# One joint small piece of 1260 columns instead of two of 840, in an L2 pooling kernel

## The chip, the cores and the metric

The kernel runs on one core of a Trainium2 chip. The metric is the device time of one execution in microseconds, lower is better. Before the change it was 394.82 us (median of 3 runs, 394.81 to 395.2). In what follows DVE is the VectorE, ACT the ScalarE, SP the SyncE. A "DMA engine" is one of the core's sixteen; a "row" is one DMA packet, the contiguous bytes of one partition (52,736 B for a load of 13184 columns).

## The reference, cut to what matters

```
x: [32, 256, 4096] float32, p = 2, kernel_size = 4
out[b, c, i] = ( mean over j < 4 of |x[b, c, 4 i + j]| ** p ) ** (1 / p)      # [32, 256, 1024]
```

Because windows of four neighbours never cross a row, the kernel treats the input as one flat list: 262144 columns on each of 128 partitions. Each element is squared, four neighbours are added, and the root of a quarter of the sum is taken. That is 134.2 MB in and 33.6 MB out, and little arithmetic.

## The kernel before

Twenty large loads go through three input buffers in turn: 18 of 13184 columns, then 12764, then 10388. ACT squares a load in place, DVE sums fours into one of two output buffers, ACT takes the root, and the result is stored, two loads to a store. The last loads are cut into chunks so that the work behind the last byte is short.

```python
W, O_W = 13184, 6592
slots = [[(W, [W])]] * 17 + [[(W, [6592, 6592])]]
slots += [[(12764, [5372, 7392])], [(10388, [6172, 2808, 1408])]]   # the last load: three chunks
ODD, ODD2 = 840, 840                                                 # the small pieces
...
# First small piece: 30 partitions x 3584 columns, the first thing that is loaded.
t = o_tiles[1][0:Q, 0:odd]                                           # Q = 30
by_load.append(nc.sync.dma_start(out=t, in_=...))
nc.vector.tensor_tensor(out=t, in0=t, in1=t, op=mult)
nc.vector.tensor_reduce(out=o, in_=t by fours, op=add)
nc.scalar.activation(out=o, in_=o, func=Act.Sqrt, scale=1.0 / k)
stores["odd"] = nc.scalar.dma_start(out=..., in_=o)                  # on the ACT queue
...
load(0)                                                              # the first large load
# Second small piece: 60 partitions (30 to 89) x 1792 columns, behind the first large load.
t2 = o_tiles[1][30:90, 0:ODD2 * P // 60]
by_load.append(nc.sync.dma_start(out=t2, in_=...))
load(1); load(2)
...                                                                  # t2 squared and summed likewise
# behind the square of load 0:
nc.scalar.activation(out=o2, in_=o2, func=Act.Sqrt, scale=1.0 / k)
stores["odd2"] = nc.sync.dma_start(out=..., in_=o2[30:90, :])        # on the SP queue
```

The small pieces hold the columns that the large loads leave over. The first is also a start: it gives the DMA engines something short to move before the first large load.

## Time and profile before

| what | before |
|---|---|
| time, median | 394.82 us |
| profiled span | 392.4 us |
| DVE busy, ACT busy | 277.4 us, 275.2 us |
| DMA over the span | 428 GB/s |
| first square on ACT begins | 20.70 us |
| last store is issued | 384.68 us |

The prediction below shows the lines and reads them. From about 6 us to 389 us the sixteen DMA engines hardly rest (16 rows or more are in flight in 99.7% of that time).

### The profile page before, as it was taken

To read this page: it belongs to the slowest core of one execution; us is meant where nothing else is said; L and a number is where in the kernel's file an instruction comes from. 1 tells how busy PE (TensorE), PEld (TensorE's weight loads), DVE (VectorE), ACT (ScalarE), POOL (GpSimd) and SP (SyncE) were. 2 spreads that over 40 slices of the span, in tenths; PEclk is the share of its full clock that TensorE was granted. 3 is DMA by queue.
4 is the path that set the end of the run, shared out by engine and by line. 5 is a ranking of instruction groups with operands and counts; after the bars stand their busy time and mean duration, and the time that the engine had idled before them with its cause. 6 is when DMAs were issued, how large, how long until landed. Compare 5 with 4: busy or idle time off the path is not lost.

```text
span 392.4 us, 186 instructions
## 1 busy us (share of the span) xinstructions
DVE 277.4 (71%) x38; ACT 275.2 (70%) x39; POOL 0.2 (0%) x4
## 2 busy tenths in 40 slices
DVE  4247698976678567856795769467947690889991
ACT  1084959927991899189908990899099909996991
POOL 0000000000000000000000000000000000000000
DMA  8999999999999999999999999999999999999997
GB/s 313 430 480 430 430 436 435 430 390 470 430 430 395 465 430 427 425 438 430 430 430 430 430 435 427 454 446 422 430 465 430 401 433 473 424 416 421 420 434 336
DMA packets 4704, 167.77 MB, mean 428 GB/s; under 512 B 556, under 2 KB 616, under 8 KB 706
## 3 DMA queue, kind: packets, MB, share of 16 engines
q1 hardware_dynamic: 3651, 144.04, 85.2%
q10 hardware_dynamic: 1053, 23.73, 14.0%
HBM read 134.22 MB, written 33.55 MB: 428 GB/s over the span
## 4 chain that ended last, share of the span: by engine, by line
DMA 50%; DVE 24%; ACT 22%; another core or an unknown queue 1%; SPq 0%; issue 0%
DMA xt<-in_x_dram 50%; ACT xt L185 21%; DVE ot L114 18%; DVE xt L125 3%; DVE xt L182 1%; ACT xt L105 1%; DVE xt L127 1%; DVE ot L127 0%; SPq L135 0%; SPq L154 0%; SPq L83 0%
## 5 line engine op out<-in xcount | busy, mean ns | idle before, releaser
L185 ACT ACTIVATE xt<-xt 128x13184 f32<-128x13184 f32 (+5 forms) x23 | 217.1, 9443 | 96.8 <-DMA xt<-in_x_dram 96.8
L114 DVE TENSOR_REDUCE ot<-xt 128x3296 f32<-128x13184 f32 x15 | 208.3, 13886 | 75.6 <-ACT xt L185 75.6
L105 ACT ACTIVATE ot<-ot 128x6592 f32<-128x6592 f32 x9 | 51.1, 5680 | 0.0
L125 DVE TENSOR_TENSOR xt<-xt 128x6592 f32<-128x6592 f32 (+6 forms) x9 | 34.1, 3786 | 16.2 <-ACT xt L185 16.0
L127 DVE TENSOR_TENSOR ot<-xt 128x3296 f32<-128x3296 f32 (+1 forms) x4 | 10.9, 2733 | 0.1
L158 DVE TENSOR_TENSOR ot<-ot 90x1792 f32<-90x1792 f32 x1 | 2.0, 2022 | 9.6 <-DMA ot<-in_x_dram 9.6
L142 ACT ACTIVATE ot<-ot 30x896 f32<-30x896 f32 x1 | 0.9, 948 | 10.7 <-DVE ot L138 10.7
L136 DVE TENSOR_TENSOR ot<-ot 30x3584 f32<-30x3584 f32 x1 | 3.9, 3878 | 4.9 <-DMA ot<-in_x_dram 4.9
L127 DVE TENSOR_TENSOR xt<-xt 128x1343 f32<-128x1343 f32 (+4 forms) x5 | 6.8, 1365 | 0.2
L105 ACT ACTIVATE xt<-xt 128x3191 f32<-128x3191 f32 (+3 forms) x4 | 5.6, 1406 | 1.2 <-DVE xt L127 1.2
L182 DVE TENSOR_TENSOR xt<-xt 128x5372 f32<-128x5372 f32 x1 | 5.7, 5748 | 0.0
L138 DVE TENSOR_REDUCE ot<-ot 30x896 f32<-30x3584 f32 x1 | 3.9, 3874 | 0.0
L159 DVE TENSOR_REDUCE ot<-ot 90x448 f32<-90x1792 f32 x1 | 2.0, 2016 | 0.0
L142 ACT ACT_TABLE_LOAD x1 | 1.3, 1283 | 0.7 <-PEq L226 0.7
L190 ACT ACTIVATE ot<-ot 90x448 f32<-90x448 f32 x1 | 0.6, 560 | 0.0
L226 POOL MEMSET const-bfloat16-1.0<- 128x1 bf16 x1 | 0.1, 102 | 0.0
L226 POOL MEMSET const-uint8-127<- 128x1 uint8 x1 | 0.1, 102 | 0.0
L226 POOL MEMSET const-float32-0.0<- 128x1 f32 x1 | 0.1, 99 | 0.2 <-issue 0.2
L226 POOL MEMSET const-float32-1.0<- 128x1 f32 x1 | 0.1, 99 | 0.0
## 6 DMA issues: line engine op xcount, KB each, us to landing
xt<-in_x_dram SPq DMA_DIRECT2D x18, 6592.0 KB, 31.3
out_dram<-ot ACTq DMA_DIRECT2D x7, 3296.0 KB, 27.2
out_dram<-ot SPq DMA_DIRECT2D x2, 3296.0 KB, 23.1
xt<-in_x_dram SPq DMA_DIRECT2D x1, 6382.0 KB, 32.0
xt<-in_x_dram SPq DMA_DIRECT2D x1, 5194.0 KB, 22.9
out_dram<-xt SPq DMA_DIRECT2D x1, 1595.5 KB, 10.8
out_dram<-xt SPq DMA_DIRECT2D x1, 1298.5 KB, 6.8
ot<-in_x_dram SPq DMA_DIRECT2D x2, 420.0 KB, 12.3
```

Of the source, the lines that this page charges most:

```text
L105: r = nc.scalar.activation(out=o, in_=o, func=Act.Sqrt, scale=1.0 / k)
L114: r = nc.vector.tensor_reduce(out=o, in_=v.rearrange("p (n j) -> p n j", j=k), axis=mybir.AxisListType.X, op=add,)
L125: r = nc.vector.tensor_tensor(out=h, in0=q[:, :, 0:2], in1=q[:, :, 2:4], op=add)
L127: r = nc.vector.tensor_tensor(out=o, in0=h[:, :, 0], in1=h[:, :, 1], op=add)
L136: nc.vector.tensor_tensor(out=t, in0=t, in1=t, op=mybir.AluOpType.mult)
L138: nc.vector.tensor_reduce(out=o, in_=t.rearrange("p (n j) -> p n j", j=k), axis=mybir.AxisListType.X, op=mybir.AluOpType.add,)
L142: nc.scalar.activation(out=o, in_=o, func=Act.Sqrt, scale=1.0 / k)
L158: nc.vector.tensor_tensor(out=t2, in0=t2, in1=t2, op=mybir.AluOpType.mult)
L159: r = nc.vector.tensor_reduce(out=o2, in_=t2.rearrange("p (n j) -> p n j", j=k), axis=mybir.AxisListType.X, op=mybir.AluOpType.add,)
L182: r = nc.vector.tensor_tensor(out=v, in0=v, in1=v, op=mybir.AluOpType.mult)
L185: r = nc.scalar.activation(out=v, in_=v, func=Act.Square)
L190: nc.scalar.activation(out=o2, in_=o2, func=Act.Sqrt, scale=1.0 / k)
```

## The change

The intent: use a shorter and better placed start. The two small pieces (840 + 840 columns) become one piece of 1260 columns, 90 rows of 7,168 B, whose first 30 rows are loaded ahead of the first large load and whose other 60 rows behind it. The piece is squared, summed, rooted and stored once. The 420 columns that are left go into the last large load, whose first chunk grows from 6172 to 6592 columns. The piece lies on partitions 2 to 91, so that its 60 rows begin at partition 32 (step 2 of the prediction has what the author estimated to gain by that). The instructions on it start at partition 0, so partitions 0 and 1 are cleared first by a memset.

```diff
-    slots += [[(12764, [5372, 7392])], [(10388, [6172, 2808, 1408])]]
-    ODD, ODD2 = 840, 840
+    slots += [[(12764, [5372, 7392])], [(10808, [6592, 2808, 1408])]]
+    ODD = 1260
...
-    (first piece: load, multiply, reduce, root, store on the ACT queue)
+    LOW, Q, FIRST = 2, 90, 30
+    odd = ODD * P // Q
+    t = o_tiles[1][:, 0:odd]
+    nc.vector.memset(t[0:LOW, :], 0.0)
+    by_load.append(nc.sync.dma_start(out=t[LOW:LOW + FIRST, :], in_=src[0:FIRST, :]))
...
         if ahead == 1:
-            t2 = o_tiles[1][30:90, 0:ODD2 * P // 60]
-            by_load.append(nc.sync.dma_start(out=t2, in_=...))
+            by_load.append(nc.sync.dma_start(out=t[LOW + FIRST:LOW + Q, :], in_=src[FIRST:Q, :]))
...
-    (second piece: multiply and reduce on partitions 0 to 89)
+    (the joint piece: multiply and reduce on partitions 0 to 91)
...
             if i == 0:
-                nc.scalar.activation(out=o2, in_=o2, func=Act.Sqrt, scale=1.0 / k)
-                stores["odd2"] = nc.sync.dma_start(out=..., in_=o2[30:90, :])
+                nc.scalar.activation(out=o_odd, in_=o_odd, func=Act.Sqrt, scale=1.0 / k)
+                stores["odd"] = nc.sync.dma_start(out=dst, in_=o_odd[LOW:LOW + Q, :])
```

More of the change, by code (lines that the diff above doesn't have):

```diff
@@ L55 @@
     n = len(loads)
-    assert sum(w for _, _, w, _ in loads) + ODD + ODD2 == total
+    assert sum(w for _, _, w, _ in loads) + ODD == total
     firsts = [sum(groups[:g]) for g in range(len(groups))]
@@ L129, in total_sum @@
         sums.append(r)
-    Q = 30
+    LOW, Q, FIRST = 2, 90, 30
     odd = ODD * P // Q
-    t = o_tiles[1][0:Q, 0:odd]
-    by_load.append(nc.sync.dma_start(out=t, in_=xf[(total - ODD) * P:total * P].rearrange("(p w) -> p w", p=Q)))
-    nc.vector.tensor_tensor(out=t, in0=t, in1=t, op=mybir.AluOpType.mult)
-    o = o_tiles[1][0:Q, odd:odd + odd // k]
-    nc.vector.tensor_reduce(
-        out=o, in_=t.rearrange("p (n j) -> p n j", j=k),
-        axis=mybir.AxisListType.X, op=mybir.AluOpType.add,
-    )
-    nc.scalar.activation(out=o, in_=o, func=Act.Sqrt, scale=1.0 / k)
-    stores["odd"] = nc.scalar.dma_start(
-        out=of[(total - ODD) * P // k:total * P // k].rearrange("(p w) -> p w", p=Q), in_=o,
-    )
+    t = o_tiles[1][:, 0:odd]
+    src = xf[(total - ODD) * P:total * P].rearrange("(p w) -> p w", p=Q)
+    dst = of[(total - ODD) * P // k:total * P // k].rearrange("(p w) -> p w", p=Q)
+    nc.vector.memset(t[0:LOW, :], 0.0)
+    by_load.append(nc.sync.dma_start(out=t[LOW:LOW + FIRST, :], in_=src[0:FIRST, :]))
     ahead = 0
@@ L150 @@
         if ahead == 1:
-            at = total - ODD - ODD2
-            t2 = o_tiles[1][30:90, 0:ODD2 * P // 60]
-            by_load.append(nc.sync.dma_start(out=t2, in_=xf[at * P:(at + ODD2) * P].rearrange("(p w) -> p w", p=60)))
-    t2 = o_tiles[1][0:90, 0:ODD2 * P // 60]
-    o2 = o_tiles[1][0:90, 4480:4480 + ODD2 * P // 60 // k]
-    nc.vector.tensor_tensor(out=t2, in0=t2, in1=t2, op=mybir.AluOpType.mult)
-    r = nc.vector.tensor_reduce(
-        out=o2, in_=t2.rearrange("p (n j) -> p n j", j=k),
+            by_load.append(nc.sync.dma_start(out=t[LOW + FIRST:LOW + Q, :], in_=src[FIRST:Q, :]))
+    t = t[0:LOW + Q, :]
+    o_odd = o_tiles[1][0:LOW + Q, odd:odd + odd // k]
+    nc.vector.tensor_tensor(out=t, in0=t, in1=t, op=mybir.AluOpType.mult)
+    sums.append(nc.vector.tensor_reduce(
+        out=o_odd, in_=t.rearrange("p (n j) -> p n j", j=k),
         axis=mybir.AxisListType.X, op=mybir.AluOpType.add,
-    )
-    sums.append(r)
+    ))
     pending = []
@@ L189 @@
             if i == 0:
-                nc.scalar.activation(out=o2, in_=o2, func=Act.Sqrt, scale=1.0 / k)
-                stores["odd2"] = nc.sync.dma_start(
-                    out=of[at * P // k:(at + ODD2) * P // k].rearrange("(p w) -> p w", p=60), in_=o2[30:90, :],
-                )
+                nc.scalar.activation(out=o_odd, in_=o_odd, func=Act.Sqrt, scale=1.0 / k)
+                stores["odd"] = nc.sync.dma_start(out=dst, in_=o_odd[LOW:LOW + Q, :])
             while held:
```

## The prediction

The range names 0.86 us for step 1; that is half of the 1.71 us that two rows of the first small load took on average (0.857 us each). In step 2, that the 39 ns over the best row (311 less 272 ns) would go with the moved partitions was the estimate.

In the kernel before, the small loads of 30 and 60 rows use fifteen of the sixteen engines, since one of the sixteen completions of each comes before any of its rows begins (at 1.30 us, first row 1.74; at 2.23 us, first row 19.80). The multiply over 1792 columns takes 2.02 us on 90 partitions. "At most some 2 us" for the memset is an estimate, to be held against that 2.02 us. In the packet records the microsecond from 5 us on lies below 400 GB/s too (357).

> **What bounds the kernel now.** I read the page's slices first, then the busy time by stretches, the timeline of the start and of the end, and last the DMA issues and the packet records behind them.
>
> The page:
>
> ```profile
> span 392.4 us, 186 instructions
> ...
> DVE 277.4 (71%) x38; ACT 275.2 (70%) x39; POOL 0.2 (0%) x4
> ...
> DMA  8999999999999999999999999999999999999997
> ...
> HBM read 134.22 MB, written 33.55 MB: 428 GB/s over the span
> ```
>
> Neither compute engine is full. The DMA row is at 9 in every slice but the first and the last. The stretches make that sharper (columns: stretch, length, DVE, ACT, POOL busy, clock, DMA share, GB/s):
>
> ```profile
> 0.00:10.00 10.00, 5.06 (x2) 1.28 (x1) 0.20 (x4) 1.00 0.92 349
> ...
> 54.00:330.00 276.00, 200.01 (x16) 200.85 (x22) 0.00 (x0) 1.00 1.00 434
> ...
> 384.00:388.00 4.00, 0.12 (x1) 0.50 (x1) 0.00 (x0) 1.00 1.02 434
> 388.00:392.00 4.00, 0.00 (x0) 0.00 (x0) 0.00 (x0) 1.00 0.59 247
> ```
>
> Between 54 and 330 us the DMA engines are at share 1.00 and 434 GB/s, and they still are at 384 to 388 us, when both compute engines are done. So the span is: time to the first packets, all bytes at about 434 GB/s, and the end of the last store. The chain of waits names DMA for 50% and compute for the rest; that is misleading, since a load that waits for the reduction three loads earlier is issued while the queue still has bytes of other loads. In the packet records I found no microsecond below 400 GB/s between 5 and 388 us but those at 20 and 21 us (389 and 397).
>
> The start, in the timeline:
>
> ```profile
> 0.73 0.45 SPq L135 DMA_DIRECT2D ot<-in_x_dram  x1
> 1.24 0.35 SPq L83 DMA_DIRECT2D xt<-in_x_dram  x1
> ...
> 4.90 3.88 DVE L136 TENSOR_TENSOR ot<-ot 30x3584 f32<-30x3584 f32 x1 [4.90 <-DMA ot<-in_x_dram]
> 8.81 3.87 DVE L138 TENSOR_REDUCE ot<-ot 30x896 f32<-30x3584 f32 x1
> ...
> 20.70 11.19 ACT L185 ACTIVATE xt<-xt 128x13184 f32<-128x13184 f32 x1 [7.03 <-DMA xt<-in_x_dram]
> 22.26 2.02 DVE L158 TENSOR_TENSOR ot<-ot 90x1792 f32<-90x1792 f32 x1 [9.57 <-DMA ot<-in_x_dram]
> 24.31 2.02 DVE L159 TENSOR_REDUCE ot<-ot 90x448 f32<-90x1792 f32 x1
> ```
>
> The reader is to see that the work on the small pieces lies in DVE time that nothing else wants: the first full reduction starts only at 31.92 us.
>
> The end:
>
> ```profile
> 368.91 5.35 ACT L185 ACTIVATE xt<-xt 128x6172 f32<-128x6172 f32 x1 [0.32 <-DMA xt<-in_x_dram]
> ...
> 374.58 3.37 DVE L125 TENSOR_TENSOR xt<-xt 128x3086 f32<-128x3086 f32 x1
> ...
> 377.58 7.43 SPq L100 DMA_DIRECT2D out_dram<-xt  x2
> ...
> 384.16 0.50 ACT L105 ACTIVATE xt<-xt 128x352 f32<-128x352 f32 x1 [0.76 <-DVE xt L127]
> ```
>
> The last store is issued at 384.68 us. Its packets begin at 385.96 on the DMA engine that is ahead and at 387.1 to 387.8 on the fifteen others, as each ends the store before it; all end between 389 and 390.94. So on the engines that finish last, the last store could be issued some 1.2 us later and cost nothing. This slack decides what the larger last chunk costs.
>
> [...] the 30 rows of the first load start as fifteen, then fifteen more, and one engine is ahead all the time. [...] the first small load's rows (14,336 B) took 0.54 to 1.19 us, mean 0.857, where a large row's pace (52,736 B in 1.955 us) would make it 0.53. [...]
>
> **The change part by part.** All sizes per DMA engine, for the fifteen that carry small pieces; 52,736 B take 1.955 us, that is 0.0371 us per 1000 B.
>
> 1. First small load: two rows of 14,336 B become two of 7,168 B. At the engine's own pace that is 14,336 B, -0.53 us. [...] But the large load behind it isn't there at once: the one engine without a small piece began it at 2.92 us, the others at 3.35 to 4.09 (mean about 3.65). They can't start much before 2.9, so the gain is between 0.5 and about 0.75. I take -0.65 us.
> 2. Second small load: the same four rows of 7,168 B, but on partitions 32 to 91 instead of 30 to 89. [...] The rows now take 272 ns at best, mean 311, up to 542. If the excess goes: 4 x 39 ns, -0.15 us.
> 3. Small stores: two of 3,584 B (140 ns) and four of 1,792 B (74 ns), 576 ns, become six of 1,792 B, 444 ns: -0.13 us.
> 4. Last load: eight rows of 41,552 B become 43,232 B: 13,440 B, +0.50 us. Last store: eight rows of 10,388 B become 10,808 B: 3,360 B, +0.12 us.
>
> Sum: -0.65 - 0.15 - 0.13 + 0.50 + 0.12 = -0.31 us. Total bytes are the same; the change moves them from a poor place to a good one. The sixteenth engine gets 0.62 us more, but it was 1.4 us or more ahead.
>
> Compute. Removed from DVE at the start: 3.88 + 3.87 us, and 0.95 us of ACT; all in idle time, worth 0. Added: a memset of 2 x 1792, at most some 2 us, while DVE waits anyway, worth 0. The joint piece's multiply and reduction keep their length (1792 elements, 2.02 us each, whatever the partitions).
>
> At the end, the last load lands at 368.9 - (0.65+0.15+0.13-0.50) = about 368.4. ACT's first chunk is 6592 instead of 6172 columns: 5.69 instead of 5.35 us, so done at about 374.1 instead of 374.25. DVE comes free at about 374.66 - 0.93 = 373.7, so it now waits for ACT. Its two adds grow from 3.37 + 1.77 to 3.59 + 1.88 us, +0.33; 374.58 becomes about 374.15, so the last issue moves by about -0.4 + 0.33 = -0.1 us. It stays inside the slack, and the stores' bytes set the end.
>
> **The rivals.**
> - Only bytes count, at the engine's pace: -0.53, 0, -0.13, +0.62 make -0.04 us, 394.8. For it: the first packets may wait for a latency that does not shrink with the row. [...]
> - The end is bound by compute: the larger chunk then costs up to 0.34 us. If the start does not help either, 395.2. Against it: DMA at 434 GB/s after compute has ended.
> - The first load waits for the memset, as both write one tile. Then everything starts up to 2 us later: 396.5. Against it: the second small load was issued at 1.64 us into the same tile with no wait for the multiply on the other partitions.
> - A second table load, since the first activation is now a square and not a root: 1.28 us on ACT at about 31 us, where ACT has 5.4 us idle before 37.76. Hidden, 0.
> - The start chain is the bound: all loads land about 0.9 us earlier and stay so, 393.9. Against it: the bytes come back in the last load.
>
> **Range and chances.** 394.82 - 0.31 gives 394.5. The known terms run from about -0.6 (0.86 and the rest in full) to +0.4 (compute rival), and the runs of before spread by 0.4, so 393.8 to 395.4 should hold it 8 times in 10. Two per cent are 7.9 us; nothing in the sum or the rivals comes near. Faster 0.01, same 0.97, slower 0.02.
>
> **What would show it.** Right: the first large load's rows start at about 3 us, not 3.65; the first square starts near 20.0 instead of 20.70, and the second near 37.0; the microseconds at 20 and 21 lose their dip; the last square of the first chunk starts at about 368.4; DMA is at 430 GB/s till the last issue plus 5 us. Wrong: the first large load's rows still start at 3.5 us or later (step 1), the small rows still take over 300 ns (step 2), DMA share sinks between 384 and 388 us (the slack was not there), or a first issue later than 0.8 us (memset).

## The result

The changed kernel takes 395.12 us (median of 6 runs, 394.71 to 395.41), the kernel before 394.81 us (6 runs of the same rounds, 394.0 to 395.2). Ratios are the mean time of one kernel's fast runs over that of the other's of the same rounds, so they are not quite the ratio of these medians: 1.0011, with a 95% interval of 0.9998 to 1.0024. A second set of rounds (run 1 below) gave 395.04 against 394.25 us, ratio 1.0019 (1.0006 to 1.0033). So the time is the same within 2%, as forecast, and inside the forecast range. But the forecast said a gain of 0.3 us, and the medians show a loss of 0.3 and 0.8 us. The first interval still holds 1, the second does not.

The page of the changed kernel, in the lines that answer to those shown of before:

```profile
span 393.6 us, 184 instructions
...
DVE 271.5 (69%) x37; ACT 276.0 (70%) x39; POOL 0.2 (0%) x4
...
DMA  8999989999999999999999999999999999999996
...
HBM read 134.22 MB, written 33.55 MB: 426 GB/s over the span
```

DVE lost 5.9 us of work and the span is longer: that work was beside the bound. DMA moved the same bytes at 426 instead of 428 GB/s. (This span is of the slowest of the six runs and the one before of a fast one. The repeated profiles below differ less, 393.3 against 392.5 us.)

The stretches (columns as in the prediction: stretch, length, DVE, ACT, POOL busy, clock, DMA share, GB/s):

```profile
0.00:10.00 10.00, 1.55 (x1) 1.28 (x1) 0.20 (x4) 1.00 0.90 359
...
384.00:388.00 4.00, 1.42 (x2) 1.36 (x3) 0.00 (x0) 1.00 0.99 421
388.00:392.00 4.00, 0.00 (x0) 0.00 (x0) 0.00 (x0) 1.00 0.58 244
```

The first 10 us moved more (359 against 349 GB/s), as intended. The end moved less (421 against 434), and both compute engines, which were nearly done at 384 us before, still have 1.4 us to do.

The timeline of the changed kernel, its start:

```profile
0.73 1.28 ACT L175 ACT_TABLE_LOAD   x1 [0.73 <-PEq L214]
0.73 0.45 SPq L140 DMA_DIRECT2D ot<-in_x_dram  x1
1.16 1.55 DVE L139 MEMSET ot<- 2x1792 f32 x1 [1.16 <-PEq L214]
1.24 0.36 SPq L83 DMA_DIRECT2D xt<-in_x_dram  x1
...
19.99 11.19 ACT L175 ACTIVATE xt<-xt 128x13184 f32<-128x13184 f32 x1 [17.98 <-DMA xt<-in_x_dram]
21.17 2.02 DVE L149 TENSOR_TENSOR ot<-ot 92x1792 f32<-92x1792 f32 x1 [18.46 <-DMA ot<-in_x_dram]
...
31.20 1.28 ACT L180 ACT_TABLE_LOAD   x1
```

The first load did not wait for the memset (both are under way at 1.16 us), and the first square begins at 19.99 instead of 20.70 us, the 0.7 us that the prediction asked for. A second table load has appeared at 31.20 us, one of the rivals.

Now follow the squares that a landing releases. Before:

```profile
37.76 11.19 ACT L185 ACTIVATE xt<-xt 128x13184 f32<-128x13184 f32 x1 [5.41 <-DMA xt<-in_x_dram]
53.36 11.19 ACT L185 ACTIVATE xt<-xt 128x13184 f32<-128x13184 f32 x1 [4.40 <-DMA xt<-in_x_dram]
...
90.52 11.19 ACT L185 ACTIVATE xt<-xt 128x13184 f32<-128x13184 f32 x1 [9.30 <-DMA xt<-in_x_dram]
```

And changed:

```profile
36.66 11.19 ACT L175 ACTIVATE xt<-xt 128x13184 f32<-128x13184 f32 x1 [3.59 <-DMA xt<-in_x_dram]
52.32 11.19 ACT L175 ACTIVATE xt<-xt 128x13184 f32<-128x13184 f32 x1 [4.47 <-DMA xt<-in_x_dram]
...
91.18 11.19 ACT L175 ACTIVATE xt<-xt 128x13184 f32<-128x13184 f32 x1 [11.00 <-DMA xt<-in_x_dram]
```

At 52 us the change is 1.04 us ahead, as much as the prediction had by then (0.93). At 91 us it is 0.66 us behind. Between the fourth square (at 69.00 instead of 70.04 us, and it waits for no landing) and the fifth, 1.7 us were lost, and ACT, which waits for nothing but the landing, shows it (11.00 us of waiting instead of 9.30). At most of the later squares the change is about 0.65 us behind, and the end is:

```profile
370.07 5.70 ACT L175 ACTIVATE xt<-xt 128x6592 f32<-128x6592 f32 x1 [0.83 <-DMA xt<-in_x_dram]
...
378.55 8.01 SPq L100 DMA_DIRECT2D out_dram<-xt  x2
...
385.70 0.50 ACT L105 ACTIVATE xt<-xt 128x352 f32<-128x352 f32 x1 [0.84 <-DVE xt L127]
```

The last load's first square begins at 370.07 instead of 368.91 us (forecast: 368.4), and the last store is issued at 386.22 instead of 384.68 us.

**One DMA engine is late.** A large load or store raises its semaphore sixteen times, once for each DMA engine, and the trace has the time of each. Work started at the sixteenth: in the kernel before, the sixteenth of the first large load came at 20.68 us and the first square began at 20.70, in the change at 19.97 and 19.99. In this table, worked out from those events, "lag" is the sixteenth less the ninth, that is how far the last engine is behind the middle one, in us. The second part is the time by which rows took longer than the engine's own pace gives for their size (1.947 us for a row of 52,736 B, 0.53 us for one of 14,336 B, which most of those rows never reach; rows under 60 ns over are left out), summed over all engines, by the time at which they began.

```
                     lag at the landing of load          end of last store    row time too much, us, begun at
kernel               first  fourth  sixth  last  store   middle    last       0-10  10-30  30-60  60-90   all
before                0.27   0.40   0.38   0.36   0.34   391.09   391.44      17.0    2.5    0.0    1.0  20.6
before, again         0.11   0.26   0.25   0.27   0.39   391.17   391.55      19.6    2.9    0.0    0.7  23.1
change                0.73   0.82   1.87   1.88   1.90   390.88   392.78      10.3    0.0    0.8    8.7  19.8
change, again         0.74   1.01   1.28   1.30   1.31   391.14   392.45      11.7    0.3    3.5   11.6  27.1
```

Three things stand there. The middle engine ends 0.1 us sooner than before on the mean of the two profiles: a gain, though a small one. The last engine ends 1.1 us later, and it ends the kernel. It begins with a lag of 0.7 us at the first load and gains more between the fourth and the sixth load, where a cluster of slow rows at 70 to 74 us has come in; in the first trace that cluster cost 0.2 to 0.6 us on most engines and 1.0 us on the one that came last. The cluster begins at 70.7 us, that is 1.6 us after the first full store is issued on the ACT queue (69.12 us) and 2.4 us before the first row of that store (73.07 us). In the kernel before, the rows in flight behind that issue show 0.6 us too much in all.

The row records do not name the engine. But a row begins within some 10 ns of the end of the row before it on its engine (put in order of time, the starts lie from 4 ns before to 3 ns after the ends in 98 of 100 rows of both kernels), so an engine that is far from the rest can be followed by these times, and the order of the rows on it is known from the program (a large load has 128 rows, eight for each engine). In the first trace of the change, the engine whose second large row begins last (6.00 us) is the one whose last row ends last (392.28 us), and its row at 71.87 us took 1.02 us too long. In the repeat it is the same (5.93 and 391.96 us, 0.93 us at 72.05), and so it is in runs 3, 6, 7 and 8 below. So the engine that is late at the start is the one that ends the kernel.

### The profile page after: what moved, and what is told of

It is laid out like the page before. It is cut to its first block, busy times and chain, and to the rows that moved or that the text cites. A ratio compares the mean times of both kernels' runs of the same rounds, so it can differ in the third digit from the quotient of the medians.

```text
span 393.6 us, 184 instructions
## 1 busy us (share of the span) xinstructions
DVE 271.5 (69%) x37; ACT 276.0 (70%) x39; POOL 0.2 (0%) x4
## 4 chain that ended last, share of the span: by engine, by line
DMA 54%; ACT 25%; DVE 19%; SPq 0%; issue 0%
DMA xt<-in_x_dram 54%; ACT xt L175 22%; DVE ot L114 14%; DVE xt L125 3%; ACT ot L105 3%; DVE ot L127 1%; DVE xt L127 1%; ACT xt L105 1%; SPq L83 0%; SPq L140 0%; SPq L146 0%
## 5 line engine op out<-in xcount | busy, mean ns | idle before, releaser
L175 ACT ACTIVATE xt<-xt 128x13184 f32<-128x13184 f32 (+4 forms) x23 | 217.4, 9457 | 108.2 <-DMA xt<-in_x_dram 108.2
L125 DVE TENSOR_TENSOR xt<-xt 128x3296 f32<-128x3296 f32 (+5 forms) x9 | 34.3, 3810 | 16.8 <-ACT xt L175 16.7
L149 DVE TENSOR_TENSOR ot<-ot 92x1792 f32<-92x1792 f32 x1 | 2.0, 2021 | 18.5 <-DMA ot<-in_x_dram 18.5
L139 DVE MEMSET ot<- 2x1792 f32 x1 | 1.6, 1552 | 1.2 <-PEq L214 1.2
L150 DVE TENSOR_REDUCE ot<-ot 92x448 f32<-92x1792 f32 x1 | 2.0, 2016 | 0.0
```

The costliest lines, as they stand in the source:

```text
L125: r = nc.vector.tensor_tensor(out=h, in0=q[:, :, 0:2], in1=q[:, :, 2:4], op=add)
L139: nc.vector.memset(t[0:LOW, :], 0.0)
L149: nc.vector.tensor_tensor(out=t, in0=t, in1=t, op=mybir.AluOpType.mult)
L150: sums.append(nc.vector.tensor_reduce(out=o_odd, in_=t.rearrange("p (n j) -> p n j", j=k), axis=mybir.AxisListType.X, op=mybir.AluOpType.a ...
L175: r = nc.scalar.activation(out=v, in_=v, func=Act.Square)
```

## The experiments

All twelve runs gave correct results, each with five rounds. The medians of before were 394.25 (first four runs), 394.49 (next four), 394.23 (next three) and 394.41 us (last one).

My first theory, A: the old kernel's small store on the ACT queue at 13.7 us was the first use of that queue; without it, the first use is a full store, and the DMA engines stumble over it. Rivals: chance (B) and the larger last chunk (C).

**1. The change again**, nothing edited.

> The changed kernel again, nothing edited. Theory A (first use of the ACT queue by a full store): in the trace of the change the rows in flight at 70 to 72 us, just as the first full store enters the ACT queue, took 6.7 us too long summed over the 16 DMA engines, one of them 1.0 us; this must come back: again about 5 to 8 us in sum at 70 to 74 us, one engine some 1 us or more behind the rest to the end, ratio to before about 1.001. Rival B (chance): the late engine and the long rows are an accident of one execution; then this profile has no such cluster at 70 us, or has it elsewhere, and the end is near 394.5. Rival C (the larger last chunk): the last store is issued at about 386.2 us again and the end is late even where no DMA engine lags.

395.04 us (394.45 to 395.38), ratio 1.0019 (1.0006 to 1.0033). The cluster is back at 71 to 74 us, the lag too, now on two engines (the fifteenth engine is 1.1 us behind the middle one at the end). So it is not chance in the sense of B: the cluster has a fixed place.

**2. The kernel before again**, nothing edited.

> The kernel before again, nothing edited, as the control. Theory A: at 70 to 74 us only the DMA engine that carries no small pieces shows a long row (0.4 us in the first trace, 0.6 us in sum), since the small store of 13.7 us has used the ACT queue on the fifteen others; no engine lags by over 0.3 us behind the fifteenth. Rival B: a lag of about 1 us on one engine may show here as well. Ratio 1.000.

394.26 us (394.04 to 394.51), ratio 1.0001 (0.9989 to 1.0014). 0.5 us of slow rows at 72 us, no late engine. The table above has it.

**3. The joint small store on the ACT queue.**

```diff
-                stores["odd"] = nc.sync.dma_start(out=dst, in_=o_odd[LOW:LOW + Q, :])
+                stores["odd"] = nc.scalar.dma_start(out=dst, in_=o_odd[LOW:LOW + Q, :])
```

> The change with one edit: the joint small store is issued on the ACT queue instead of the SP queue, so that fifteen DMA engines have used the ACT queue at about 33 us. Theory A: the cluster of long rows at 70 us shrinks from 6.7 us to under 1.5 us in sum, the late engine gains about 1 us, the time falls by 0.4 to 1.2 us against the change, ratio to before 0.998 to 0.9995. Rival B: same as the change within 0.3 us with long rows where chance puts them. Rival C: same as the change, last issue at 386 us.

395.26 us (395.02 to 395.63), ratio 1.0027 (1.0015 to 1.0040). The ACT queue was in use from 33 us on, and the cluster, at 70 to 76 us, was larger, not smaller: 14.6 us.

**4. The kernel before with its first small store on the SP queue.**

```diff
-    stores["odd"] = nc.scalar.dma_start(out=..., in_=o)      # right behind the root
...
     (loads 0, 1, 2 and the second small load are issued)
+    stores["odd"] = nc.sync.dma_start(out=..., in_=o)
```

> The kernel before with one edit: its first small store is issued on the SP queue behind the first loads instead of on the ACT queue, so that the first use of the ACT queue is the first full store at 70 us. Theory A: the cluster of long rows at 70 to 74 us appears (5 to 8 us in sum) and the time rises by 0.3 to 1.2 us, ratio 1.001 to 1.003. Rival B and rival C: no change, ratio 1.000, since neither the sizes nor the last chunk differ from before.

394.36 us (394.25 to 395.01), ratio 1.0007 (0.9994 to 1.0019). The first use of the ACT queue is now a full store at 70 us, and there is no slow row at 68 to 76 us at all. Theory A has fallen in both directions.

What was left: the sizes (E: a shorter first piece), the joint store or the moved partitions (F), the second table load (G). I undid or did them one at a time.

**5. The sizes alone**, in the structure of before.

```diff
-    slots += [[(12764, [5372, 7392])], [(10388, [6172, 2808, 1408])]]
-    ODD, ODD2 = 840, 840
+    slots += [[(12764, [5372, 7392])], [(10808, [6592, 2808, 1408])]]
+    ODD, ODD2 = 420, 840
```

> The kernel before with the sizes of the change alone: the first small piece is 420 columns (30 rows of 7,168 B, partitions 0 to 29), the last load has 10808 columns; the two pieces are still worked and stored apart, the first stored on the ACT queue, partitions and the single table load as before. What is to be explained: all three kernels with the change's start have 7 to 15 us of row time too much (sum over 16 DMA engines) at 70 to 75 us, the three with the old start 0 to 0.6 us there; and one or two engines begin the first large load 0.3 to 0.7 us after the rest. Theory E (the shorter first piece no longer covers the time in which the rows of the first large load reach the DMA engines, so that they start unevenly, and the late ones stay late): this kernel has both, one or two late engines at 5 to 6 us and the cluster at 70, and a time 0.4 to 1.0 us above before (ratio 1.001 to 1.0025). Theory F (the joint store, or the moved partitions) and theory G (the second table load): no cluster and no late engine, time 0.2 to 0.6 us below before (ratio about 0.999).

395.09 us (394.36 to 395.46), ratio 1.0007 (0.9992 to 1.0023). By the ratio alone that would be unclear: in the rounds of runs 5 to 8 the kernel before itself spread from 394.14 to 396.18 us, so their four ratios, 1.0005 to 1.0011, all have 1 in their intervals, and what follows rests on the traces. The trace is not: the last engine is 0.6 us behind from the second load on and 1.13 us at the end (last landing 392.49 us), as in the change and unlike before. In the timeline, the first square and that of the last load:

```profile
20.84 11.19 ACT L185 ACTIVATE xt<-xt 128x13184 f32<-128x13184 f32 x1 [12.29 <-DMA xt<-in_x_dram]
...
369.86 5.70 ACT L185 ACTIVATE xt<-xt 128x6592 f32<-128x6592 f32 x1 [0.84 <-DMA xt<-in_x_dram]
```

The cluster, however, was not at 70 us as I had expected of E; 12.6 us of slow rows were at 18 to 21 us, where the second small load with its old partitions lies. So even the first square came no sooner than before (20.84 us). In this one trace the new sizes bring the late engine, without the joint store, the moved partitions or the second table load.

**6. One table load.**

```diff
     nc.vector.memset(t[0:LOW, :], 0.0)
+    nc.scalar.activation(out=t[0:LOW, 0:8], in_=t[0:LOW, 0:8], func=Act.Sqrt, scale=1.0 / k)
```

> The change plus one tiny square root on the two cleared partitions ahead of all other activations, so that the set with the root is loaded first and there should be one table load, not two. Theory G (second table load): the cluster at 70 to 75 us goes and the time falls by 0.5 to 1 us against the change. Theories E and F: one table load fewer, the rest stays as in the change, ratio to before 1.001 to 1.003.

395.22 us (394.79 to 395.34), ratio 1.0009 (0.9993 to 1.0025). The table load behind the first square is gone; the one at 0.73 us, now for the root on the two partitions, is the only one:

```profile
19.83 11.19 ACT L176 ACTIVATE xt<-xt 128x13184 f32<-128x13184 f32 x1 [16.88 <-DMA xt<-in_x_dram]
30.93 0.56 ACT L181 ACTIVATE ot<-ot 92x448 f32<-92x448 f32 x1
```

The root follows the square at once, without the 1.28 us load between them. The cluster (9.6 us at 60 to 90 us) and the lag at the end (1.60 us) stay. Theory G falls.

**7. The piece on partitions 0 to 89.**

```diff
-    LOW, Q, FIRST = 2, 90, 30
+    LOW, Q, FIRST = 0, 90, 30
-    nc.vector.memset(t[0:LOW, :], 0.0)
```

> The change with its piece on partitions 0 to 89 instead of 2 to 91, so without the memset. Prediction's step 2 [...]: the rows of the second small load take over 300 ns again with a dip at 20 us, some 0.1 to 0.2 us lost. Theory F in its form of the partitions: the cluster at 70 us and the late engine go, time 0.3 us below before. Theories E and G: cluster and late engine stay, ratio to before 1.001 to 1.003.

395.09 us (394.26 to 395.41), ratio 1.0005 (0.9989 to 1.0021). The rows of the second small load took 339 ns on average, in the change 274 ns and in the kernel before 311 ns: step 2 of the prediction was right about the time. The lag at the end is 1.83 us. Here the slow rows were at 18 to 21 us (5.9 us) and at 60 to 90 us (3.4 us).

**8. Two small stores, as before.**

```diff
-                stores["odd"] = nc.sync.dma_start(out=dst, in_=o_odd[LOW:LOW + Q, :])
+                stores["odd"] = nc.scalar.dma_start(out=dst[0:FIRST, :], in_=o_odd[LOW:LOW + FIRST, :])
+                stores["odd2"] = nc.sync.dma_start(out=dst[FIRST:Q, :], in_=o_odd[LOW + FIRST:LOW + Q, :])
```

> The change with the small result stored in two parts as before, 30 rows on the ACT queue and 60 on the SP queue. Theory F in its form of the joint store: the cluster at 70 us goes, time 0.3 us below before. Theories E and G: cluster and late engine stay, ratio to before 1.001 to 1.003.

395.09 us (394.72 to 395.71), ratio 1.0011 (0.9995 to 1.0027). Cluster (9.6 us) and lag at the end (1.54 us) stay. With runs 7 and 8 theory F falls, in both its forms. The late engine started here with a lag of only 0.43 us, and collected the rest later, some of it in single rows at 150 and 324 us (0.45 and 0.51 us).

So E was left: by it the first piece is a cover, which must keep the DMA engines busy until the first large load's rows have reached all of them. The row records of the start show why that may fail: the first rows of one load do not begin on all engines at once (with nothing ahead, in run 10, between 1.75 and 3.37 us). Before, fifteen engines finished their two small rows between 3.3 and 4.1 us, and the one engine without small rows could begin its large row only at 2.92 us (2.75 and 2.84 us in the other two profiles of the old start). In the change the small rows were done at 2.6 to 3.0 us, and the second large row of the middle engine began at 5.15 us, but that of the last engine at 6.00 us (before: 6.03 and 6.26). That is a gain of 0.9 us for the middle and 0.26 us for the last. On that last engine the first large row began 0.11 us after all small rows had ended, and it took 2.93 us, where the middle one took 2.3. In run 3, two engines began it 0.68 and 0.78 us after all small rows had ended, and these two were the late ones. In run 12 every first large row begins within 0.02 us of the end of a small row. So the missing cover is seen plainly in run 3; in the change itself most of the lag is a slow first row, and why that row is slow is not shown. The next four runs change only how and in which order the small rows are loaded.

**9. All 90 small rows ahead of the first large load.**

```diff
-    by_load.append(nc.sync.dma_start(out=t[LOW:LOW + FIRST, :], in_=src[0:FIRST, :]))
+    by_load.append(nc.sync.dma_start(out=t[LOW:LOW + Q, :], in_=src))
...
-            by_load.append(nc.sync.dma_start(out=t[LOW + FIRST:LOW + Q, :], in_=src[FIRST:Q, :]))
```

> The change with only the order of the small loads altered: all 90 rows in one load ahead of the first large load, six rows of 7,168 B for each of fifteen DMA engines instead of two. So far every kernel with the short first piece (two rows of 7,168 B, 0.54 us at the engine's pace) has one or two DMA engines late by 0.4 to 1.0 us at the landing of the first large load and by 1.0 to 1.9 us at the end, and the kernels with the long first piece (two rows of 14,336 B) have none. Theory E (the first piece must last until the rows of the first large load have reached the last DMA engine; an engine that starts late stays late and loses more later): six rows, 1.6 us, cover it; the last engine is under 0.5 us behind the median from the first load to the end, no cluster at 70 to 75 us, time 0.2 to 1.0 us below the change, ratio to before 0.998 to 1.0005. Rival H (the late engine comes from the 420 columns more in the last load, or from rows of 7,168 B as such, not from the order): the last engine is still over 1 us behind at the end, time as the change, ratio 1.001 to 1.002.

394.6 us (394.38 to 394.92), ratio 1.0009 (0.9997 to 1.0022). No slow row after 10 us, and the lag does not grow: 0.64 us at the first load, 0.70 us at the end. The lag is not under 0.5 us as E had it, and the ratio misses E's 1.0005: the cover itself ran unevenly, with 25.8 us of slow rows in the first 10 us, so that the first large rows began between 3.5 and 5.5 us. The last landing is 392.02 us.

**10. All 90 small rows behind the first large load**, so no cover.

```diff
-    by_load.append(nc.sync.dma_start(out=t[LOW:LOW + FIRST, :], in_=src[0:FIRST, :]))
...
-            by_load.append(nc.sync.dma_start(out=t[LOW + FIRST:LOW + Q, :], in_=src[FIRST:Q, :]))
+            by_load.append(nc.sync.dma_start(out=t[LOW:LOW + Q, :], in_=src))
```

> The change with all 90 small rows in one load behind the first large load, so nothing covers the start. Theory E: the DMA engines start the first large load as its rows reach them, spread over 0.5 us or more; one or more engines are late by 0.4 us or more at its landing and by over 1 us at the end; time as the change or up to 0.5 us more, ratio to before 1.000 to 1.002. If they start evenly instead, the uneven start comes from the short piece ahead and not from the rows' arrival. Rival H: late engine as in the change.

395.43 us (395.22 to 395.62), ratio 1.0030 (1.0016 to 1.0044), the slowest of all. With nothing ahead of it, the large load's first rows began between 1.75 and 3.37 us, though it was issued at 0.73 us: by E this spread is what a cover has to hide. The lag is 1.23 us at the first load and 0.9 us at the end (E had over 1 us), and 23.3 us of slow rows lie at 18 to 21 us, where the 90 small rows came.

**11. The first small load on the ACT queue**, so that the first large load is issued at 0.73 us.

```diff
-    by_load.append(nc.sync.dma_start(out=t[LOW:LOW + FIRST, :], in_=src[0:FIRST, :]))
+    by_load.append(nc.scalar.dma_start(out=t[LOW:LOW + FIRST, :], in_=src[0:FIRST, :]))
```

> The change with its first small load issued on the ACT queue, so that the first large load is issued on the SP queue at 0.73 us instead of 1.24 us. Theory E: the large load's rows reach the last DMA engine some 0.5 us earlier, while the small rows are still moving; the late engine's lag falls under 0.5 us, no cluster at 70 us, and time falls by 0.5 to 1.2 us against the change, ratio to before 0.9975 to 0.9995. Rival H: the start moves by up to 0.5 us but one engine is still over 1 us behind at the end, ratio 1.000 to 1.001. It may also be that rows of the two queues mix on each engine and the small piece lands later; that costs nothing by the timeline, since its work has 10 us of idle DVE time.

395.33 us (395.13 to 395.81), ratio 1.0030 (1.0018 to 1.0043). A miss: the rows of the large load got ahead of the small ones (the first small row began at 4.20 us), so the cover was gone and not better timed. Lag 0.86 us at the first load and 0.88 us at the end, with 28.9 us of slow rows at the start.

**12. The two small loads exchanged**: 60 rows ahead, 30 behind.

```diff
-    by_load.append(nc.sync.dma_start(out=t[LOW:LOW + FIRST, :], in_=src[0:FIRST, :]))
+    by_load.append(nc.sync.dma_start(out=t[LOW + FIRST:LOW + Q, :], in_=src[FIRST:Q, :]))
...
-            by_load.append(nc.sync.dma_start(out=t[LOW + FIRST:LOW + Q, :], in_=src[FIRST:Q, :]))
+            by_load.append(nc.sync.dma_start(out=t[LOW:LOW + FIRST, :], in_=src[0:FIRST, :]))
```

> The change with its two small loads exchanged: the 60 rows on partitions 32 to 91 go ahead of the first large load, the 30 rows on 2 to 31 behind it. Ahead of the large load there are now four rows of 7,168 B for each of fifteen DMA engines, 1.09 us at the engine's pace [...], so the cover should end at about 3.3 us, after the rows of the large load have reached most engines. Theory E (cover): the last engine is under 0.5 us behind the median at the first large load's landing and under 0.7 us at the end, last landing of all stores near 391.3 to 391.9 us against 392.45 to 392.86 in the kernels with the short piece or none ahead; time 0.3 to 1.0 us below the change's 395.04 to 395.12, ratio to before 0.9985 to 1.0007. Rival H (the 420 columns more at the end cost what they cost, whatever the start): ratio 1.001 to 1.002, last engine over 1 us behind at the end. This is also the version that the runs so far point to, should one beat both kernels.

394.4 us (393.92 to 395.11) against 394.41 us, ratio 0.9996 (0.9984 to 1.0009). The time is back at that of before, with all else as in the change, the 420 columns in the last load, the joint store and the second table load too. So rivals C and H, by which the larger last load costs what it costs, fall. E was right on the end (0.43 us), not on the first load, where it had the last engine under 0.5 us behind (0.61). The timeline:

```profile
20.17 11.19 ACT L175 ACTIVATE xt<-xt 128x13184 f32<-128x13184 f32 x1 [18.15 <-DMA xt<-in_x_dram]
...
89.86 11.19 ACT L175 ACTIVATE xt<-xt 128x13184 f32<-128x13184 f32 x1 [9.58 <-DMA xt<-in_x_dram]
...
368.74 5.70 ACT L175 ACTIVATE xt<-xt 128x6592 f32<-128x6592 f32 x1 [0.85 <-DMA xt<-in_x_dram]
...
377.21 8.01 SPq L100 DMA_DIRECT2D out_dram<-xt  x2
```

The fifth large square begins at 89.86 us, 1.3 us sooner than in the change, and the last load's at 368.74 instead of 370.07 us. The same measures as above, for all the variants:

```
                     lag at the landing of load          end of last store    row time too much, us, begun at
kernel               first  fourth  sixth  last  store   middle    last       0-10  10-30  30-60  60-90   all
4  before, SP store   0.35   0.21   0.20   0.33   0.32   391.36   391.67      20.7    4.7    0.0    0.1  25.7
3  ACT store          0.93   0.95   1.45   1.47   1.37   391.16   392.53      10.2    0.0    0.0   14.6  24.8
6  root first         0.64   0.87   1.61   1.69   1.60   390.99   392.58      10.2    0.0    1.1    9.6  21.3
7  partitions 0-89    0.74   0.74   1.36   1.82   1.83   390.94   392.77      10.4    5.9    0.7    3.4  20.9
8  two stores         0.43   0.60   0.65   1.51   1.54   391.17   392.71      11.2    1.3    4.1    9.6  27.2
5  sizes alone        1.42   0.62   0.63   1.26   1.13   391.36   392.49      11.5   12.6    0.0    0.0  25.0
10 none ahead         1.23   0.85   0.85   0.95   0.90   391.96   392.86       8.8   23.3    0.0    0.0  32.3
11 30 on ACT queue    0.86   0.85   0.88   0.85   0.88   391.57   392.45      28.9    0.0    0.0    0.0  28.9
9  90 ahead           0.64   0.67   0.68   0.66   0.70   391.32   392.02      25.8    0.0    0.0    0.0  25.8
12 60 ahead           0.61   0.41   0.42   0.40   0.43   391.00   391.42       7.4   12.2    0.0    0.4  20.0
```

Run 12 and the first trace of the change have the same sum of slow rows (20.0 and 19.8 us) and nearly the same middle engine (391.00 and 390.88 us). They differ in the last engine, 391.42 against 392.78 us. That is the loss.

No version beat both kernels: run 12 equals before within its interval and is below the change (1.0011 and 1.0019 in other rounds). It shared no round with the change, so its lead of some 0.6 us is a comparison by way of the kernel before, and the intervals of the ratios overlap (0.9984 to 1.0009 against 0.9998 to 1.0024 and 1.0006 to 1.0033). Run 12 also changes two things at once: four rows for each engine ahead instead of two, and two behind instead of four. How late the last engine starts, behind the middle one, can be read at the second large row: 0.1 to 0.2 us in the kernel before, 0.2 us in run 12, 0.85 us in the change, 0.66 us in run 9, 0.85 us in run 10 and 1.36 us in run 11. So only run 12 removes the late start. That the lag grows later is another matter: it does not grow in runs 9, 10 and 11, though they start late too. There E, by which late engines lose more, failed.

## Why the prediction was right or wrong

The range and the chances held, but they do not speak for the sum: the range was 1.6 us wide, five times the forecast gain, and the result lies near its upper end, by the rival at 395.2. The sign did not hold. The early signs that the prediction named came true (large rows begin at 2.54 to 3.08 us, first square at 19.99, second at 36.66), but they tell of the start and not of the last engine; the sign at the end (368.4) did not. These are the steps.

- **Bound by DMA: right, but in the wrong form.** The prediction had "all bytes at about 434 GB/s". That is the mean of sixteen engines. The end is set by the last one, and the mean hid it: two kernels whose middle engines end within 0.2 us of each other differ by 1.1 us.
- **Step 1, the first small load (-0.65 us): the step that failed.** It counted one gain for "the fifteen that carry small pieces". It had the limit in hand ("the large load behind it isn't there at once", 2.92 us) and used it as a floor for all alike. The floor was no floor (rows began from 2.54 us on), and the gain was not one for all. Measured at the second large row, the middle engine gained 0.9 to 1.0 us (6.03 to 5.15, and 6.12 to 5.09 in the repeats) and the last one 0.26 to 0.31 us (6.26 to 6.00, 6.24 to 5.93). With -0.26 in place of -0.65, the prediction's own sum is +0.08 us instead of -0.31.
- **Step 2, the moved partitions (-0.15): right.** Rows of the second small load went from 311 and 318 ns on average to 274 and 273 ns, which is 0.15 to 0.18 us for four. Why they are shorter there is not shown.
- **Step 3, the small stores (-0.13): not separated.** The run with two stores was no slower or faster than the change.
- **Step 4, the larger last load and store (+0.50, +0.12): right.** Rows of 43,232 B took 1.60 us against 1.54, rows of 10,808 B 0.41 against 0.395, eight of each.
- **Not in the sum at all: slow rows at 70 to 74 us.** They gave back what the start had saved. Slow-row time in the first 10 us fell from 17.0 and 19.6 to 10.3 and 11.7 us; at 60 to 90 us it rose from about 1 to 8.7 and 11.6 us. Over sixteen engines that is 0.4 to 0.5 us saved and 0.5 to 0.7 us lost, and the late engine lost more than the others.
- **Compute at the end.** The chunk took 5.70 us as forecast, and DVE did wait for ACT. But all of it began 1.7 us later than forecast, since the last engine's rows of the last load were late, and the last store was issued at 386.22 instead of about 384.6 us. This follows the late engine; in run 12, with the same chunk, the last issue was at 384.89 us.
- **The rivals.** The memset held nothing up. The second table load came and was hidden, as said. The chain rival did not happen. The compute rival (395.2) came closest to 395.12, but by luck: the engine that ended last began its rows of the last store at 389.02 us, 2.8 us after the issue, so the issue did not hold it up. "Only bytes count" (-0.04 us) had the sign wrong too.
- **A reading.** The fifteen engines begin the last store at 387.29 us or later, not at 387.1 (that is the fourth row of the engine ahead). The slack is as the prediction had it.

What is shown, by the traces: the loss sits in one or two late DMA engines; in the change the engine that is late at the start ends the kernel; the new sizes alone bring a late engine (one trace); loading the 60 small rows ahead and the 30 behind removes the late start and the growth, with the rest of the kernel kept (one trace, run 12). What is only argued: that the short piece fails because the large load's rows have not reached the engine yet, and that the cover's length decides, not the number of small rows behind the first load. What stays open: why the slow rows come in a cluster at a fixed place (18 to 21 us in some variants, 70 to 75 us in others, within the first 10 us in the rest), and why an engine that is out of step loses more than the rest in the change and not in runs 9 to 11. Neither the use of the queue, nor the store's form, nor the table load, nor the partitions alone decided it.

## What to carry to other kernels

When the DMA engines are saturated, look at the last engine and not at the mean rate: the sixteen completion times of a load show whether one is late, and one that starts late can stay late for the whole kernel (lags of 0.4 to 0.9 us at the first load became 1.3 to 1.9 us at the end in the change and runs 3 and 6 to 8; 0.64 us became 0.70 in run 9). In this kernel a small load ahead of the first large one seems to have worked as a cover for the time in which the large one's first rows begin (1.75 to 3.37 us with nothing ahead, run 10), which is argued and not shown; before you cut such a load, look whether it still outlasts that time on every engine. Where the terms of a sum are a few tenths of a microsecond and of both signs, ask for each whether it holds for the slowest engine too.
